# Running both mixers before both feed-forward stages in a two-block trunk kernel

## The chip, the cores and the metric

The kernel runs on one core of a Trainium2 chip. The metric is the device time of one execution in microseconds, as the median of several runs. The engines are named as in the profile: PE (matrix multiplications), DVE, ACT and POOL (elementwise work), SP (issues transfers).

## The reference, cut to what matters

One layer over 2048 rows of width 1024, all in float32:

```python
def reference(x, ...):
    for l in range(L):                       # L = 1
        xn = rmsnorm(x, norm1_g[l])
        z = xn @ w_in[l]
        u_pool, zq, zf, zi, zo, zg = split(z)
        gates = sigmoid(zg + b_gate[l])      # two gates of width 1024
        ya = pool_mixer(u_pool, ...) @ w_pa[l]
        yb = hgrn2_mixer(zq, zf, zi, zo, ...) @ w_pb[l]
        x = x + (gates[:, 0] * ya + gates[:, 1] * yb) @ w_o[l]
        x = x + conv_glu_ffn(rmsnorm(x, norm2_g[l]), ...)   # w_up, causal conv of width 3, SiLU gate, w_down
    return rmsnorm(x, final_g)
```

The pooling, the recurrence of `hgrn2_mixer` and the convolution look only backwards along the rows, so a later block needs states and last rows of an earlier one, and no FFN result is needed by a mixer (there is one layer).

## The kernel before, in words

The rows are worked on as two super-blocks of 1024 rows, `b0` = 0 and 2, each made of two halves of 512 rows (blocks 0, 1 and 2, 3). A super-block goes through `mixer(b0)` and `ffn(b0)`, and the program runs mixer 0, FFN 0, mixer 2, FFN 2.

Inside `mixer`, the input projections come first (tiles `io`, `fr`, `gr` and others), beside them the tasks of the pooling and of the recurrence. Their results are spilled to DRAM as `md` and `od` and come back as `mx` and `oT`, which the branch projections `pa` and `pb` split into a high and a low part (`mxs_0h`, `mxs_0l`, `oTs_0h` and so on). The output projection `wo` follows, in seven products in the order P1, P6, P5, P7, P4, P3, P2. After P4 the finished rows x + mixer of the first half exist, after P2 those of the second. `ffn` has the up-projection (`up`), the convolution and gate, and the down-projection (`dn`), again in seven products, the last ones P4 and P3, each followed by the final norm of its rows.

Each large product of super-blocks is done by seven smaller products over sums of operands, and each of those by three matrix multiplications over high and low parts. The weights come through one stream in the order in which the products use them: SP loads `raw` (8 buffers), ACT casts it to the high part (L205) and DVE subtracts for the low part (L206), both into `ops`. The order of this stream is written down ahead by `plan_mixer` and `plan_ffn`.

Sums of weights that the products of `wo`, `up` and `dn` need are built in DRAM by transfers alone (`Sums.make`, started by `prepare`): a copy on ACT's queue (L278) or an accumulating transfer on POOL's (L275), 1 MB in most steps, ten groups of eight steps, two groups at a time. `wo` is `sw`, `up` is `su0` to `su5`, `dn` is `sd0` to `sd2`. After a step the builder waits `SUM_LAG` ticks, where a tick is six matrix multiplications. It starts after the first `io` projection.

The next stage's operands are made while the last products of a stage run. `forms_of(kind, b, ...)` makes them in two tasks (first half and second half): `norm_rows` takes the root of the mean square of each row (on ACT, `row_rstd`, L626, with a few small steps on POOL), scales the row with it on DVE (L640), PE transposes it (L646) and ACT copies it back with the norm's gain (L654); then come the splits (L597 on ACT, L598 on DVE). `"x"` is the operand of a mixer and `"m"` that of an FFN. In before, `forms_of("m", b0)` begins in `wo` behind P7 and takes its rows from SBUF; `spill_rows` stores them to DRAM afterwards (`dx`), since `dn` adds them later. `forms_of("x", b0 + 2)` begins in `dn`'s P3 at k = 1, where `load_rows` fetches x (L501), and again at k = 4 for the second half. `go_io` and `go_up` let the second half's transposes begin.

All tiles of 512 columns share a ring of 77 buffers (`slot`), and the engines' instructions run on each engine in the order in which the program writes them.

Of the kernel before, what the change touches and what calls it, by code (L numbers as in the profile page):

```python
# [11 lines left out]
F32 = mybir.dt.float32  # L12
# [59 lines left out]
SUM_LAG = 7  # L72
# [6 lines left out]
def tile_trunk(  # L79
# [409 lines left out]
    for n in range(SEQ // SB):  # L489
        plan_mixer(n)  # L490
        plan_ffn()
# [13 lines left out]
    def load_rows(b):  # L505
        for j in range(NT):
            load_x_tile(b, j)
# [122 lines left out]
    def norm_rows(src, name, xs, after, lag=1):  # L630
        for j in range(NT):
            while (src, j) not in ready:
                yield 1
            halves = [xt[src, j, c] for c in range(2)]
            t = [slot(f"{name}xs{j}_{hf}") for hf in range(2)]
            r = row_rstd(halves, t, f"{name}{j}")
            if lag:
                yield lag
            for hf in range(2):
                dve.tensor_scalar(t[hf], halves[hf], r[:, 0:1], None, ALU.mult)  # L640
                xs[j, hf] = t[hf]
            after(j)
# [14 lines left out]
    def spill_rows(b):  # L657
        def after(j):
            for hf in range(2):
                t = xt.pop((("m", b), j, hf))  # L660
                d = dram.tile([P, 512], F32, tag=f"dx{b}_{j}_{hf}", name=f"dx{b}_{j}_{hf}")
                sp.dma_start(d, t)
                x2d[b, j, hf] = d
        return after

    def forms_a_task(src, gain, forms, full, after=lambda j: None, early=False):
# [4 lines left out]
        def rows(j):  # L671
            after(j)
            if early:
                for k in range(KD):
                    transpose(pts[k], xs, j, k)
# [10 lines left out]
    def forms_b_task(src, gain, forms, full, after, go):  # L686
        name = f"{src[0]}{src[1]}_"
        xs = {}
        yield from norm_rows(src, name, xs, after, 0)
# [54 lines left out]
    def forms_of(kind, b, gain, after=lambda b: lambda j: None, early=False, go=lambda: True):  # L744
        forms = {k: [] for k in ("B11", "B21", "B22", "T1", "T2", "T3", "T4")}
        full = {k: [] for k in ("B11", "B21", "T2")}
        first = Task(forms_a_task((kind, b), gain, forms, full, after(b), early))
        late = Task(forms_b_task((kind, b + 1), gain, forms, full, after(b + 1), go))
        return forms, first, late
# [408 lines left out]
    def mixer(b0, forms, late):  # L1158
# [172 lines left out]
        def ready_rows(hf):  # L1331
            def done(j):
                for c in range(2):
                    xt[("m", b0 + hf), j, c] = acc[hf, j, c]
                ready.add((("m", b0 + hf), j))
# [11 lines left out]
        go_up[0] = False  # L1347
        return nxt
# [3 lines left out]
    def ffn(b0, forms, late):  # L1352
# [162 lines left out]
        go_io[0] = False  # L1515
# [73 lines left out]
```

## Time and profile before

| | |
|---|---|
| time, median of 3 runs | 2622.06 us (2621.85 to 2622.27) |
| profiled execution, first to last instruction | 2614.3 us |
| around the span, median less span | 7.8 us (the profile gives no time of its own for the execution beside the span) |
| mean granted clock of TensorE | 0.989 |
| PE busy | 2533.7 us, 97% |
| DVE, ACT, POOL busy | 75%, 45%, 35% |
| HBM read, written | 384.94 MB, 187.17 MB |

The stages by PE's timeline, from the start of the span: mixer 0 from 16 to 671 us (`pa` from 464.5, `wo` from 579.5), FFN 0 to 1339 (`dn` from 1111), mixer 2 to 1950 (`pa` from 1763, `wo` from 1865), FFN 2 to 2606 (`dn` from 2389), and the last rows' norm to 2614.

The busy line tells only that PE has nearly no time to spare over the whole. Where it has some is read from stretches: two stages that do the same work in the two super-blocks can be laid side by side, and what differs between them is a wait or the clock. In a timeline row, the bracket at the end holds the idle time of that engine before the instruction and what ended it. DMA landing times run from the issue to the last byte.

### The profile page before, as it was taken

What the parts mean: (1) busy time and instruction counts of PE and PEld (TensorE: products, weight loads), DVE (VectorE), ACT (ScalarE), POOL (GpSimd) and SP (SyncE); (2) the same over time, 40 slices, a digit from 0 to 9 for tenths busy, and PEclk for the clock granted to TensorE, in tenths of its full rate; (3) what the DMA queues carried; (4) which work ended last, traced back from release to release, by engine and by line L of the source; (5) the groups of instructions that cost most, each with busy time, mean ns of one, the idle gap of its engine ahead of it and who ended that gap; (6) DMA issues with size and microseconds to landing.
All of it is one profiled execution on the core that took longest, in us unless ns stands there. A gap on an engine that the chain in (4) does not pass through costs nothing. (4 is left out here: it accounts for less than half of the span.)

```text
span 2614.3 us, 35569 instructions
## 1 busy us (share of the span) xinstructions
PE 2533.7 (97%) x11464; PEld 2064.8 (79%) x11464; DVE 1967.4 (75%) x3390; ACT 1168.9 (45%) x2204; POOL 909.3 (35%) x1253
## 2 busy tenths in 40 slices
PE   7899999989999999999999999999999999999998
PEld 6788888767778888878878788887787888887887
DVE  7898779358799877876476787774778987787845
ACT  5333434224555544555364344442345554445633
POOL 5544343062444343362141111200623433335402
PEclk9999999999999999999999999999999999999999
DMA  6887868888778897587365344346452445545943
GB/s 221 274 213 211 224 189 242 268 275 214 198 188 241 243 240 198 165 305 255 108 195 157 101 135 121 116 145 218 142 173 84 151 150 148 141 141 185 377 142 105
DMA packets 254059, 496.90 MB, mean 190 GB/s; under 512 B 26736, under 2 KB 43248, under 8 KB 253552
## 3 DMA queue, kind: packets, MB, share of 16 engines
q1 hardware_dynamic: 187968, 319.89, 38.9%
q0 software_dynamic: 41504, 110.64, 16.6%
q10 hardware_dynamic: 24400, 64.08, 7.1%
q8 instruction: 91, 1.49, 0.2%
q14 instruction: 96, 0.79, 0.1%
HBM read 384.94 MB, written 187.17 MB: 219 GB/s over the span
## 5 line engine op out<-in xcount | busy, mean ns | idle before, releaser
L205 ACT CAST ops<-raw 128x512 fp32r<-128x512 f32 x732 | 451.6, 620 | 780.1 <-PE dn_P L145 141.1
L206 DVE TENSOR_TENSOR ops<-raw,ops 128x512 fp32r<-128x512 f32 x732 | 564.1, 775 | 214.2 <-ACT ops L205 208.7
L1381 DVE SCALAR_TENSOR_TENSOR e<-h,cols,e 128x512 f32<-128x512 f32 x176 | 142.4, 813 | 29.9 <-ACT e L1379 26.1
L1379 ACT ACTIVATE e<-h,cols 128x512 f32<-128x512 f32 x176 | 142.6, 814 | 24.2 <-DVE h L984 16.9
L1384 DVE SCALAR_TENSOR_TENSOR e<-h,cols,e 128x512 f32<-128x512 f32 x176 | 133.9, 769 | 3.0
L796 POOL DMA_DIRECT2D g_P<-dg_P x154 | 83.7, 545 | 107.6 <-PE dn_P L145 70.0
L1090 POOL TENSOR_TENSOR gf_P<-e,e 128x512 f32<-128x512 f32 x44 | 67.8, 1542 | 153.1 <-DVE e L1390 97.8
L1090 POOL TENSOR_TENSOR gf_P<-gf_P,e 128x512 f32<-128x512 f32 x44 | 60.1, 1366 | 68.5 <-DVE e L1390 68.1
L1374 POOL COPY h<-h 128x2 f32<-128x2 f32 x88 | 40.7, 482 | 113.9 <-DVE h L982 112.0
L1301 POOL TENSOR_TENSOR ya<-ya,gl 128x512 f32<-128x512 f32 x32 | 45.8, 1460 | 98.4 <-issue 49.1
L1376 POOL COPY hist<-h 128x2 f32<-128x2 f32 x88 | 35.3, 401 | 127.3 <-DVE h L984 125.6
L1234 ACT ACTIVATE gt<-gt,cols 128x512 f32<-128x512 f32 x48 | 34.8, 724 | 90.5 <-DVE gt L984 71.1
L1388 ACT ACTIVATE e<-e 128x512 f32<-128x512 f32 x88 | 55.5, 631 | 37.9 <-DVE e L1384 37.4
L984 DVE TENSOR_TENSOR h<-up_u,up_V 128x512 f32<-128x512 f32 x88 | 60.2, 684 | 15.2 <-PE up_V L145 14.8
L1197 POOL TENSOR_TENSOR q<-q,qs 128x512 f32<-128x512 f32 x16 | 22.5, 1407 | 136.0 <-ACT qs L1196 105.0
L846 POOL COPY qm<-q 128x64 f32<-128x64 f32 x64 | 22.4, 367 | 117.0 <-DVE q L852 21.6
L1066 DVE TENSOR_TENSOR x<-x,wo_P 128x512 f32<-128x512 f32 x88 | 56.4, 690 | 6.2 <-PE wo_P L145 6.1
L1066 DVE TENSOR_TENSOR ac<-ac,dn_P 128x512 f32<-128x512 f32 x72 | 46.6, 683 | 13.4 <-PE dn_P L145 13.3
L1404 POOL DMA_DIRECT2D dg_P<-gf_P x88 | 52.5, 596 | 10.9 <-POOL gf_P L1090 6.5
L1450 POOL TENSOR_TENSOR fss<-fss 128x1 f32<-128x1 f32 x16 | 4.6, 289 | 141.5 <-ACT fj L1439 141.5
L619 POOL TENSOR_SCALAR ro<-so 128x4 f32<-128x4 f32 x16 | 5.2, 323 | 135.6 <-ACT sq L956 135.4
L1018 ACT COPY up_e<-up_X 128x512 f32<-128x512 f32 x44 | 25.8, 586 | 56.7 <-PE up_X L145 51.6
(1265 smaller groups left out, 8332.4 us busy)
## 6 DMA issues: line engine op xcount, KB each, us to landing
g_P<-dg_P POOLq DMA_DIRECT2D x154, 256.0 KB, 6.2
raw<-in_w_up_t SPq DMA_DIRECT2D x132, 256.0 KB, 3.3
raw<-in_w_in_t SPq DMA_DIRECT2D x98, 256.0 KB, 3.3
dg_P<-gf_P POOLq DMA_DIRECT2D x88, 256.0 KB, 3.9
raw<-in_w_io SPq DMA_DIRECT2D x68, 256.0 KB, 4.9
dg_P<-e SPq DMA_DIRECT2D x66, 256.0 KB, 3.3
raw<-in_w_dn SPq DMA_DIRECT2D x66, 256.0 KB, 3.0
x<-in_x SPq DMA_DIRECT2D x64, 256.0 KB, 5.3
```

What stands on the lines that cost most here:

```text
L205: self.mark = act.copy(hi, v)
L206: dve.tensor_tensor(lo, v, f32(hi), ALU.subtract)
L796: eng.dma_start(t, d)
L984: dve.tensor_tensor(dst, t, ps, ALU.add if how == "add" else ALU.subtract)
L1066: dve.tensor_tensor(t, t, ps[j], ALU.add if sg > 0 else ALU.subtract)
L1090: pin(pool.tensor_tensor(t, x0, x1, op))
L1301: pool.tensor_tensor(y[m, hf], y[m, hf], g, ALU.add)
L1379: in_turn(act.activation(t, h[:, 2:], AF.Identity, bias=col(o_cb + mt), scale=col(o_cw + 4 * MF + mt)))
L1381: in_turn(second(dve.scalar_tensor_tensor(t, h[:, 1 : 1 + TB], col(o_cw + 2 * MF + mt), t, ALU.mult, ALU.add)))
L1384: dve.scalar_tensor_tensor(t, h[:, 0:TB], col(o_cw + mt), t, ALU.mult, ALU.add)
L1388: in_turn(act.activation(g, g, AF.Silu))
L1404: pool.dma_start(d, t)
```

## The change

The main loop runs the two mixers first and then the two FFNs, and the weight stream is planned in that order. `wo` of the first mixer is now followed by `io` of the second, `wo` of the second by `up` of the first FFN, and `dn` of the first by `up` of the second. Finished rows no longer stay in SBUF for the FFN: `keep_rows` takes the root of each row tile as soon as the tile is done, copies it into a small tile that stays on chip (`rs2`, 128x16), and stores the rows to DRAM. `norm_rows` for `"m"` fetches them and scales them with the kept root. The next operands begin in `wo` at P4, k = 0 (`begin`), for the first mixer x of block 2 with block 3's loads at P3, k = 0 (`begin2`), for the second the rows of block 0. In `dn` of the first FFN, `each3` begins the rows of block 2 in place of x. `SUM_LAG` goes from 7 to 11.

```diff
-SUM_LAG = 7
+SUM_LAG = 11
...
     for n in range(SEQ // SB):
         plan_mixer(n)
+    for n in range(SEQ // SB):
         plan_ffn()
...
     def norm_rows(src, name, xs, after, lag=1):
+        kind, b = src
         for j in range(NT):
-            while (src, j) not in ready:
+            if kind == "m":
+                halves = [fetch(x2d[b, j, c], f"{name}r{j}_{c}") for c in range(2)]
+                t, r = halves, rs2[:, b * NT + j : b * NT + j + 1]
                 yield 1
-            halves = [xt[src, j, c] for c in range(2)]
-            t = [slot(f"{name}xs{j}_{hf}") for hf in range(2)]
-            r = row_rstd(halves, t, f"{name}{j}")
-            if lag:
-                yield lag
+            else:
+                ...
             for hf in range(2):
-                dve.tensor_scalar(t[hf], halves[hf], r[:, 0:1], None, ALU.mult)
+                dve.tensor_scalar(t[hf], halves[hf], r, None, ALU.mult)
...
+    rs2 = const.tile([P, SEQ // P], F32, tag="rs2", name="rs2")
+
+    def keep_rows(b, j, halves):
+        junk = [slot(f"mj{b}_{j}_{c}") for c in range(2)]
+        r = row_rstd(halves, junk, f"m{b}_{j}")
+        pool.tensor_copy(rs2[:, b * NT + j : b * NT + j + 1], r[:, 0:1])
+        for c in range(2):
+            d = dram.tile([P, 512], F32, tag=f"dx{b}_{j}_{c}", name=f"dx{b}_{j}_{c}")
+            sp.dma_start(d, halves[c])
+            x2d[b, j, c] = d
...
+        def begin(k):
+            if k == 0:
+                if last:
+                    nxt.append(forms_of("m", 0, o_n2, go=lambda: go_up[0]))
+                else:
+                    load_rows(b0 + 2)
+                    nxt.append(forms_of("x", b0 + 2, o_n1, go=lambda: go_io[0]))
+
+        def begin2(k):
+            if k == 0 and not last:
+                load_rows(b0 + 3)
...
         wo.run("P7", 2)
-        nxt = forms_of("m", b0, o_n2, spill_rows, go=lambda: go_up[0])
-        wo.run("P4", 2, done=ready_rows(0))
-        wo.run("P3", 2)
-        wo.run("P2", 3, done=ready_rows(1))
-        go_up[0] = False
-        return nxt
+        go_io[0] = go_up[0] = False
+        wo.run("P4", 2, begin, rows_done(0))
+        wo.run("P3", 2, begin2)
+        wo.run("P2", 3, done=rows_done(1))
+        return nxt[0]
...
         def each3(k):
             if k == X_AT and not last:
-                load_rows(b0 + 2)
-                nxt.append(forms_of("x", b0 + 2, o_n1, go=lambda: go_io[0]))
-            if k == X_AT2 and not last:
-                load_rows(b0 + 3)
+                nxt.append(forms_of("m", b0 + 2, o_n2, go=lambda: go_up[0]))
...
-    for b in range(0, SEQ // TB, 2):
-        forms, task, late = nxt
-        join(task)
-        forms, task, late = mixer(b, forms, late)
-        join(task)
-        nxt = ffn(b, forms, late)
+    for stage in (mixer, ffn):
+        for b in range(0, SEQ // TB, 2):
+            forms, task, late = nxt
+            join(task)
+            nxt = stage(b, forms, late)
```

What the change does to the order of instructions shows in three places. Line numbers of the changed kernel are some eight higher there; a name's number behind the last underscore only tells tiles apart, and `mxs1_2h` is the split of the third `mx` tile of block 1.

The first is ACT at the first mixer's `pa`, where the reloaded tiles are split while copies of weight sums (`su`) are issued. Before:

```order
L597 CAST mxs1_0h_4836<-mx1_0_4834 128x512
L205 CAST ops131_4940<-raw117_4632 128x512
L278 DMA su1s4_3375<-su1s2_3373 16x16384
L956 ACTIVATE sq0_3_4855,so0_3_4856<-po0_3_4846 128x128 x4
L1234 ACTIVATE gt0_1_7_4876<-gt0_1_7_4876,cols_84 128x512
L791 DMA gd0_1_7_4879<-gt0_1_7_4876 128x512
L205 CAST ops132_5003<-raw118_4634 128x512
L278 DMA su2s4_3497<-su2s2_3495 16x16384
L597 CAST mxs1_1h_4894<-mx1_1_4892 128x512
L1234 ACTIVATE gt1_0_7_4904<-gt1_0_7_4904,cols_84 128x512
L791 DMA gd1_0_7_4907<-gt1_0_7_4904 128x512
L597 CAST mxs1_2h_4911<-mx1_2_4909 128x512
```

And the same place in the changed kernel:

```order
L205 CAST ops131_4931<-raw117_4620 128x512
L278 DMA su1s3_4551<-in_w_up_t 512x1x512
L598 CAST mxs1_0h_4827<-mx1_0_4825 128x512
L964 ACTIVATE sq0_3_4846,so0_3_4847<-po0_3_4837 128x128 x4
L1242 ACTIVATE gt0_1_7_4867<-gt0_1_7_4867,cols_84 128x512
L205 CAST ops132_4994<-raw118_4622 128x512
L799 DMA gd0_1_7_4870<-gt0_1_7_4867 128x512
L598 CAST mxs1_1h_4885<-mx1_1_4883 128x512
L1242 ACTIVATE gt1_0_7_4895<-gt1_0_7_4895,cols_84 128x512
L799 DMA gd1_0_7_4898<-gt1_0_7_4895 128x512
L598 CAST mxs1_2h_4902<-mx1_2_4900 128x512
```

Two copies stood between the first and the third split, and now one stands ahead of the first.

The second is ACT at the end of the first `wo`, where P2's splits stand among the squares of rows. Before, the squares were those of finished rows (`m0`):

```order
L626 ACTIVATE m0_xs2_0_6239,m0_2ss_6241<-x0_2_0_5443 128x512
L626 ACTIVATE m0_xs2_1_6240,m0_2ss_6241<-x0_2_1_5445 128x512
L597 CAST wo0_P2_0h_6253<-ya1_4_5044 128x512
L205 CAST ops168_6306<-raw154_6066 128x512
L626 ACTIVATE m0_xs3_0_6274,m0_3ss_6276<-x0_3_0_5487 128x512
L626 ACTIVATE m0_xs3_1_6275,m0_3ss_6276<-x0_3_1_5489 128x512
L597 CAST wo0_P2_1h_6296<-ya1_5_5132 128x512
L205 CAST ops169_6331<-raw155_6092 128x512
L597 CAST wo0_P2_2h_6317<-ya1_6_5259 128x512
```

In the changed kernel the squares of block 3's x, which wait for loads, stand there:

```order
L627 ACTIVATE x3_xs0_0_6360,x3_0ss_6362<-x3_0_0_6329 128x512
L627 ACTIVATE x3_xs0_1_6361,x3_0ss_6362<-x3_0_1_6331 128x512
L627 ACTIVATE x3_xs1_0_6371,x3_1ss_6373<-x3_1_0_6333 128x512
L627 ACTIVATE x3_xs1_1_6372,x3_1ss_6373<-x3_1_1_6335 128x512
L627 ACTIVATE x3_xs2_0_6382,x3_2ss_6384<-x3_2_0_6337 128x512
L627 ACTIVATE x3_xs2_1_6383,x3_2ss_6384<-x3_2_1_6339 128x512
L205 CAST ops171_6506<-raw157_6112 128x512
L278 DMA su1s4_4552<-su1s2_4550 16x16384
L627 ACTIVATE x3_xs3_0_6393,x3_3ss_6395<-x3_3_0_6341 128x512
L205 CAST ops172_6546<-raw158_6149 128x512
L627 ACTIVATE x3_xs3_1_6394,x3_3ss_6395<-x3_3_1_6343 128x512
L598 CAST wo0_P2_2h_6410<-ya1_6_5248 128x512
```

Eight squares of freshly loaded rows and one copy now stand ahead of the split `wo0_P2_2h`. They come from the end of the first `dn`, where before eight squares of `x3` stood between `dn0_P3_9h` and `dn0_P3_10h`; there the changed kernel has

```order
L598 CAST dn0_P3_9h_18416<-g0_P3_9_18228 128x512
L598 CAST dn0_P3_10h_18437<-g0_P3_10_18272 128x512
L205 CAST ops575_18522<-raw561_18287 128x512
L661 ACTIVATE m2_b0_18474<-m2_t0_18469,cols_84 128x512
L205 CAST ops576_18631<-raw562_18318 128x512
```

with the two splits side by side.

The third is POOL at the second mixer's `pb`, where `ro` belongs to the end of the recurrence and `ya` is the first merge of a branch. Before:

```order
L619 TENSOR_SCALAR ro2_3_16895<-so2_3_16890 128x4
L620 TENSOR_TENSOR ro2_3_16895<-ro2_3_16895,neghalf_116 128x4
L619 TENSOR_SCALAR ro3_3_17005<-so3_3_17000 128x4
L620 TENSOR_TENSOR ro3_3_17005<-ro3_3_17005,neghalf_116 128x4
L1301 TENSOR_TENSOR ya2_0_17008<-ya2_0_17008,gl2_1_0_17365 128x512
```

In the changed kernel:

```order
L620 TENSOR_SCALAR ro2_3_10819<-so2_3_10814 128x4
L621 TENSOR_TENSOR ro2_3_10819<-ro2_3_10819,neghalf_116 128x4
L275 DMA su5s1_10172<-in_w_up_t 256x1x512
L620 TENSOR_SCALAR ro3_3_10929<-so3_3_10924 128x4
L621 TENSOR_TENSOR ro3_3_10929<-ro3_3_10929,neghalf_116 128x4
L275 DMA sd0s1_10359<-in_w_dn 512x1x512
L275 DMA su5s3_10174<-in_w_up_t 256x1x512
L275 DMA sd0s3_10361<-in_w_dn 512x1x512
L1309 TENSOR_TENSOR ya2_0_10932<-ya2_0_10932,gl2_1_0_11292 128x512
```

Four accumulating transfers have moved here, three of them together.

More of the change, by code (lines that the diff above doesn't have):

```diff
@@ L655, in transposed, with forms_a_task @@
         return t
[L657 to L666, printed above, removed]
+    rs2 = const.tile([P, SEQ // P], F32, tag="rs2", name="rs2")
[7 more added lines that the diff above has]
+            x2d[b, j, c] = d
+    def forms_a_task(src, gain, forms, full, early=False):
         name = f"{src[0]}{src[1]}_"
@@ L684, in forms_a_task, with forms_b_task @@
             forms[key].append(split(t, f"{name}f{k}", True))
-    def forms_b_task(src, gain, forms, full, after, go):
+    def forms_b_task(src, gain, forms, full, go):
         name = f"{src[0]}{src[1]}_"
         xs = {}
-        yield from norm_rows(src, name, xs, after, 0)
+        yield from norm_rows(src, name, xs, lambda j: None, 0)
         while not go():
```

25 lines of the change are left out of this document (15 added, 10 removed).

## The prediction

> **What bounds the kernel now.** I read the busy line of the page first, then the busy times by stage, then the list of waits, and last the timeline around each long wait. The profiled span is 2614.3 us; the runs have a median of 2622.06 us, 7.8 us more, which lies around the span and which I leave as it is. So a microsecond off the span is a microsecond off the time.
>
> ```profile
> PE 2533.7 (97%) x11464; PEld 2064.8 (79%) x11464; DVE 1967.4 (75%) x3390; ACT 1168.9 (45%) x2204; POOL 909.3 (35%) x1253
> ```
>
> TensorE is the bound, and the change leaves its 11464 matmuls alone. What can move is the idle rest, 81 us, and the stretches at half clock behind it. The stages (start:end, length, busy of PE, PEld, DVE, ACT, POOL, granted clock, DMA share, GB/s) show where they lie:
>
> ```profile
> 464.50:671.00 206.50, 187.47 (x814) 149.59 (x813) 131.66 (x198) 68.71 (x142) 69.20 (x69) 0.97 0.86 254
> 1111.20:1338.80 227.60, 221.02 (x957) 178.99 (x956) 143.25 (x223) 111.77 (x216) 80.80 (x140) 0.99 0.67 227
> 1763.40:1950.30 186.90, 181.04 (x814) 146.56 (x813) 123.69 (x194) 66.97 (x140) 61.05 (x61) 1.00 0.55 178
> 2389.40:2606.00 216.60, 214.84 (x925) 173.40 (x923) 134.67 (x204) 99.44 (x186) 72.53 (x121) 1.00 0.60 208
> ```
>
> Rows one and three are the same work (pa, pb and wo, 814 matmuls): the first mixer needs 19.6 us more, at a DMA share of 0.86 against 0.55. Rows two and four are the down-projections: the first needs 11.0 us more. In PE's timeline (start, length, instruction, in brackets the idle time before it and what ended it) these are the longest waits outside io, and below them the list of all that PE waits for in the second mixer's pa, pb and wo (us in total, times, longest):
>
> ```profile
> 486.57 0.80 PE L145 MATMUL pa<-mxs_2h,ops 128*128 128x512 f32 x1 [5.83 <-ACT mxs_2h L597]
> 534.22 0.49 PE L145 MATMUL pb<-oTs_0h,ops 128*128 128x512 f32 x1 [4.01 <-ACT oTs_0h L597]
> 585.83 1.53 PE L145 MATMUL wo_P<-ops,wo_P_0l 128*128 128x512 f32 x4 [4.16 <-DVE wo_P_0l L598]
> 1331.59 3.78 PE L145 MATMUL dn_P<-ops,dn_P_10h 128*128 128x512 f32 x8 [4.14 <-ACT dn_P_10h L597]
> ...
> PE wo_P L145 <- DVE x L1066: 2.9, 2, 1.6
> PE pt L968 <- DVE ot L962: 1.7, 1, 1.7
> PE wo_P L145 <- ACT wo_P_0h L597: 1.2, 1, 1.2
> ```
>
> The first three lie in the first mixer's pa, pb and wo, and the second mixer has none of them. The fourth is at the end of dn0, where x of the next super-block is loaded.
>
> **The contention in the first mixer.** The reloads mx and oT (md and od in DRAM back to SBUF) feed pa and pb. Four answers on these tiles, in the order mx first mixer, mx second, oT first, oT second:
>
> ```profile
> DMA to landing us min/median/max: 3.1/8.5/10.5
> ...
> DMA to landing us min/median/max: 3.4/3.7/5.5
> ...
> DMA to landing us min/median/max: 5.5/6.3/9.7
> ...
> DMA to landing us min/median/max: 3.6/4.1/5.4
> ```
>
> What else is under way: the copies of the weight sums (L278, 1 MB each) and the accumulates on POOL (L275). Their issue times (first and last start) and an accumulate's landing:
>
> ```profile
> L278 ACTq DMA_DIRECT2D su1s<-su1s x2: 476/508/540, 421.9 to 472.1; - x2
> L278 ACTq DMA_DIRECT2D su2s<-su2s x2: 475/486/497, 429.8 to 475.4; - x2
> L278 ACTq DMA_DIRECT2D su3s<-in_w_up_t x2: 550/570/590, 516.3 to 542.3; - x2
> L278 ACTq DMA_DIRECT2D su4s<-in_w_up_t x2: 566/568/571, 523.4 to 550.6; - x2
> ...
> DMA to landing us min/median/max: 3.9/6.7/10.1
> sd0s<-in_w_dn POOLq DMA_DIRECT2D x4, 1024.0 KB, 12.2
> ```
>
> The pa wait that ends at 486.57 stands behind copies issued at 472.1 and 475.4, the pb wait that ends at 534.22 behind copies issued at 516.3 and 523.4. In the second mixer the sums are long done.
>
> **The change part by part.**
>
> T1, dn0's end. The timeline of ACT and then of PE:
>
> ```profile
> 1324.24 0.63 ACT L626 ACTIVATE x_xs<-x 128x512 f32<-128x512 f32 x1 [2.30 <-DMA x<-in_x]
> 1324.78 0.19 ACT L626 ACTIVATION_READ_ACCUMULATOR x_xs<-x 128x1 f32 x1
> 1330.94 0.60 ACT L597 CAST dn_P_10h<-g_P 128x512 fp32r<-128x512 f32 x1
> ...
> 1323.58 0.60 PE L646 MATMUL x_t<-ident,x_xs 128*128 128x128 f32 x4
> 1323.93 0.72 PE L145 MATMUL dn_P<-ops,dn_P_8l 128*128 128x512 f32 x2
> 1324.49 2.04 PE L145 MATMUL dn_P<-ops,dn_P_9h 128*128 128x512 f32 x8
> ```
>
> The split dn_P_10h stands behind eight squares of x3, and the first waits for a load. The changed kernel has no squares here: 16 fetches of finished rows and 16 DVE scalings by a root that is on chip, and dn_P_10h directly behind dn_P_9h. The wait of 4.14 goes, with the half clock behind it (eight matmuls took 3.78 after it and 2.04 before). Against dn2, dn0 has 32 transposes more, some 2.8 us at 0.35 for four (1323.58 to 1323.93); 11.0 less 2.8 leaves 8.2 as the most to gain. Nothing is gained if the fetches come as late as x did. In place of x, finished rows are now late if anything is, and then PE waits for their transposes. I take -7, ends -8.2 and 0.
>
> T2, wo0's end. This is where the x loads, 16 squares and 16 scalings now are, so what is taken from dn0 comes here. The eight x3 loads stand on SP behind the stores of the finished rows, and eight x3 squares stand on ACT ahead of the splits wo0_P2_2h and 2h's follower 3h. Behind those wait the casts of the weights and then PE. From before: the last of the eight row stores of the first half, the cast that must now wait, and the first matmul that needs it; then the landing of x and of the row stores:
>
> ```profile
> 646.98 1.61 SPq L662 DMA_DIRECT2D dx<-x  x3
> 649.85 0.61 ACT L597 CAST wo_P_2h<-ya 128x512 fp32r<-128x512 f32 x1
> 661.13 0.62 PE L145 MATMUL wo_P<-ops,wo_P_2h 128*128 128x512 f32 x2
> ...
> DMA to landing us min/median/max: 4.3/5.5/6.5
> ...
> DMA to landing us min/median/max: 2.0/6.0/14.0
> ```
>
> x3 is issued from 648.6 on; with 5.5 us the first lands at 654 and, at eight squares of 0.63 and their read-outs of 0.19, the split starts at 661 and PE waits about 0.5 to 1.5; with the 14.0 that one store took it waits about 9. I take +2.5, nearer the median than the maximum, ends 0 and +10.
>
> Does a wait of 2 us also cost clock? Two waits in the second mixer's projections, and the two windows of 3.4 us around the later one:
>
> ```profile
> 1447.23 1.13 PE L895 MATMUL pl<-q,k 128*128 128x128 f32 x8 [1.21 <-DVE q L820]
> 1450.00 0.77 PE L145 MATMUL gr_X<-x_f4h,ops 128*128 128x512 f32 x1 [1.64 <-ACT gr_e L1018]
> ...
> 1446.80:1450.20 3.40, 1.33 (x9) 1.17 (x10) 3.40 (x8) 2.67 (x7) 0.00 (x0) 0.98 0.75 200
> 1450.20:1453.60 3.40, 3.40 (x9) 2.66 (x10) 3.40 (x10) 0.03 (x1) 0.32 (x1) 0.52 0.24 70
> ```
>
> PE is busy for 1.33 of 3.40, and the next 3.4 us run at a granted clock of 0.52: 1.6 us lost. I count that half window for each wait of T2, T4 and T5. The Trainium skill ("TensorE: Matmul & The Clock Gate", section on HAM oscillation) puts the rule as no PE-idle gaps above about 3.4 us; by that rule T2's wait would cost no clock and the sum would be some 1.5 us lower, but this row shows the clock falling after gaps that are each at most half as long, so the row decides.
>
> T3, wo2's end. m0 and m1 are fetched back from DRAM, 16 fetches of 256 KB, on SP behind the row stores. In the second mixer's wo the DMA share is low (0.55 over the row above), and x_b and square work is the same as before. 0, ends -1 and +3. The chain of transposes and T2 forms at the start of both up-projections stands as it did, so its waits stay.
>
> T4, thinner sums in the first mixer. A step now comes every 11 ticks instead of 7. Between mxs_0h and wo's first split ACT had six copies, now three, and none among the oT splits. The window behind the pa wait, and DVE ahead of the wo wait:
>
> ```profile
> 487.60:491.00 3.40, 3.40 (x9) 2.60 (x9) 3.11 (x8) 1.17 (x6) 0.00 (x0) 0.51 0.73 265
> ...
> 579.00 4.28 DVE L206 TENSOR_TENSOR ops<-raw,ops 128x512 fp32r<-128x512 f32 x1 [1.04 <-ACT ops L205]
> ```
>
> pa: 5.8 of wait and, at 0.51 from 486.57 to 491, about 2.2 of clock; one copy ahead in place of two, landing between 8.5 and 3.7, so 3 stays: -5. pb: 4.0 and 1.7; no copy near, oT lands near 4.1 and was 6.3: -4.5. wo: 4.2 and 1.7 come from the weight subtraction of 4.28 us on DVE, which the order of both engines still allows: -2. Sum -11.5, taken as -11; ends 0 and -19.6, the whole difference of rows one and three.
>
> T5, the same sums in the second mixer. They now run through it and into up0. Copies stand before mxs2_0h and mxs2_1h, none before mxs3 or among the oT splits; but three accumulates stand together on POOL ahead of pb2, and two copies ahead of wo2. Half of what pb lost in the first mixer, 3, and 1 for wo: +4; ends 0 and +19.6.
>
> Edits that I cost at nothing: 32 more fetches (8 MB, issued at the two stage ends of T1 and T3, where their landing is counted), 16 root copies of 128x1 on POOL (35% busy), the other order of weights in the stream, and the missing x-square wait at io2. Squares, scalings and stores are as many as before. If their cover goes, it shows in T1 to T3.
>
> Sum: -7 + 2.5 + 0 - 11 + 4 = -11.5; span 2602.8, time 2610.5 us.
>
> **The rivals.**
>
> R1, one copy delays a reload as long as two do. For: the second copy was issued 3.3 us after the first, less than the shortest landing of 3.9, so the two overlapped for most of the wait. Then pa keeps its wait, T4 is -6 and the time 2615.5. The Trainium skill ("DMA: Bandwidth & Descriptors", section on queues, rings and completion order) says each DMA engine takes turns between the queue rows that have work; by that, one copy on ACT's row slows SP's reload as much as two. Against: the second mixer without copies waits for nothing, so a shorter overlap should gain something.
>
> R2, dn0's stall moves whole to wo0. The order there is the same (eight x3 squares ahead of a split), and loads there landed later. T2 is then +9, the time 2617, no change that can be told.
>
> R3, slower. Three accumulates, each about 12 us to land, stand on POOL ahead of the oT reloads of the second mixer. If these land as late as the 14.0 of the slowest store, 10 above their 4.1, pb waits about 10 at each of its two halves, and with 1.7 of clock each and 3 for pa and wo T5 is +26: 2632.5. It decides from T5 at +20.7. Against: in the first mixer accumulates also stood there and cost far less.
>
> R4, all contention goes: T4 -19.6, T5 0, the time 2598.
>
> **How the numbers follow.** 0.2%, 5.2 us, is about what a measurement of this kernel can tell from no change. Forecast (2604 to 2615) 0.45, R1 0.13, R2 0.13, R3 0.14, R4 0.15. Faster takes R4, half of R1 (which lies at the bound) and the forecast but 0.05 for its upper tail: 0.60. Same takes R2 and those two rests: 0.24. Slower is R3 and 0.02 for several ends at once: 0.16. The range goes from 2599, beside R4, to 2629, between before and R3.
>
> **What would show it.** T1: no wait for dn_P_10h, dn0 near 220 us. T2: a wait for wo_P_2h below 3 us. T4: pa to wo of the first mixer near 195 us, oT landing near 4. T5: the second near 191. It is wrong if the second mixer shows the waits for mxs or oTs that the first had, or if wo0 waits above 6.

## The result, and the profile after

The changed kernel takes 2650.86 us (median of 4 runs, 2646.61 to 2654.49) against 2621.95 us of the kernel before beside it: 1.0112 times as long, 95% interval 1.0097 to 1.0126. That is 28.9 us slower; the forecast was 11.5 us faster, and the time lies above its range.

The profiled execution took 2654.49 us with a span of 2652.8, so 1.7 us lie around the span. The 38.5 us between the two spans are therefore more than the 28.9 between the medians: this execution was 3.6 us above its median, and the profiled one of before, if 1.7 us lay around its span too, some 6 us below. Stage lengths come from one execution of each kernel, so a difference of a few us between two of them can be that of the executions.

The busy line of the page after:

```profile
PE 2544.8 (96%) x11464; PEld 2065.4 (78%) x11464; DVE 1973.7 (74%) x3390; ACT 1166.7 (44%) x2202; POOL 915.8 (35%) x1269
```

PE executes the same 11464 matmuls and is busy for 11.1 us more than before: that part of the 38.5 is matmuls at a lower clock or with operands that come late, the rest is idle time. The stages of after, in the order first projections, pa to wo of the first mixer, pa to wo of the second, dn0, up2, dn2 (same columns as in the prediction):

```profile
119.80:479.10 359.30, 344.47 (x1718) 285.59 (x1716) 288.68 (x670) 135.45 (x304) 132.97 (x145) 0.99 0.63 185
479.10:686.70 207.60, 185.29 (x814) 147.13 (x812) 138.07 (x198) 73.65 (x163) 77.20 (x87) 0.97 0.79 235
1111.80:1318.70 206.90, 189.90 (x814) 149.51 (x813) 133.63 (x207) 68.83 (x144) 71.17 (x75) 0.95 0.73 222
1758.90:1978.30 219.40, 217.65 (x957) 176.65 (x956) 140.85 (x220) 100.31 (x181) 69.76 (x114) 1.00 0.68 233
1978.30:2426.70 448.40, 437.35 (x1884) 351.96 (x1883) 369.64 (x516) 227.05 (x373) 163.70 (x248) 0.99 0.47 142
2426.70:2644.30 217.60, 214.45 (x925) 173.20 (x923) 134.12 (x204) 99.50 (x186) 72.41 (x121) 1.00 0.61 207
```

And two stages of before that the prediction did not show, the first projections and up2:

```profile
116.20:464.50 348.30, 341.43 (x1717) 284.43 (x1716) 287.39 (x667) 134.09 (x302) 140.81 (x151) 1.00 0.80 221
1950.20:2389.40 439.20, 434.82 (x1882) 351.58 (x1881) 363.19 (x510) 223.99 (x362) 156.34 (x237) 1.00 0.47 141
```

Against before, dn0 is 8.2 us shorter, as said. The first projections are 11.0 longer, the first mixer's pa to wo 1.1 longer instead of 11 shorter, the second's 20.0 longer, and up2 9.2 longer. The long waits of PE in after:

```profile
600.93 2.08 PE L145 MATMUL wo_P<-ops,wo_P_0l 128*128 128x512 f32 x4 [12.29 <-DVE wo_P_0l L599]
...
1136.20 0.79 PE L145 MATMUL pa<-mxs_3h,ops 128*128 128x512 f32 x1 [5.80 <-ACT mxs_3h L598]
...
1981.79 0.50 PE L145 MATMUL up_X<-m_f1l,ops 128*128 128x512 f32 x1 [2.30 <-DVE m_f1l L599]
...
1991.31 0.76 PE L145 MATMUL up_X<-m_f4h,ops 128*128 128x512 f32 x1 [4.30 <-ACT up_e L1026]
```

**The wait of 12.29 at wo0.** Before it was 4.16. DVE and then POOL in after, just ahead of it:

```profile
563.68 9.51 DVE L206 TENSOR_TENSOR ops<-raw,ops 128x512 fp32r<-128x512 f32 x1
...
579.53 0.69 DVE L1301 TENSOR_TENSOR gl<-gl,pb 128x512 f32<-128x512 f32 x1 [5.74 <-DMA gl<-gd]
...
583.00 4.00 DVE L206 TENSOR_TENSOR ops<-raw,ops 128x512 fp32r<-128x512 f32 x1
...
595.37 0.69 DVE L1301 TENSOR_TENSOR gl<-gl,pb 128x512 f32<-128x512 f32 x1 [7.17 <-DMA gl<-gd]
...
599.25 1.62 DVE L599 TENSOR_TENSOR wo_P_0l<-ya,wo_P_0h 128x512 fp32r<-128x512 f32 x1
```

```profile
561.47 1.14 POOL L275 DMA_DIRECT2D su1s<-in_w_up_t  x1
562.14 1.80 POOL L1098 TENSOR_TENSOR yf_P<-ya,ya 128x512 f32<-128x512 f32 x1
...
569.61 3.01 POOL L1098 TENSOR_TENSOR yf_P<-ya,ya 128x512 f32<-128x512 f32 x2
```

A weight subtraction, which takes 0.68 us where nothing holds it, took 9.51. It began 1.5 us into a run of eight additions on POOL that followed an accumulate's issue, and ended 0.56 us after the last of them (572.63). A second one, at 583.00, took 4.00: it followed the accumulate that POOL issued at 581.53, and it too ended 0.56 us after the last of POOL's three additions there (586.45). Behind each of them everything is in order: the next weight load on SP waits for that subtraction's buffer, and gates `gl` stand behind the load. SP's issues:

```profile
559.15 14.38 SPq L182 DMA_DIRECT2D raw<-sw0s  x2
...
577.57 9.78 SPq L182 DMA_DIRECT2D raw<-sw0s  x2
...
588.40 0.86 SPq L804 DMA_DIRECT2D gl<-gd  x2
```

And of the list of SP's waits from 537 to 605 us (total, times, longest) the first row:

```profile
SPq L182 <- DVE ops L206: 37.7, 7, 13.7
```

SP waited up to 13.7 us (7.3 at the same place before), until the first hold ended at 573.19. The gates behind that load were issued at 574.5 to 577.0, DVE waited 5.74 for one, and only then came to the subtraction of 4.00. The next load waited for this one until 587.0, the gates behind it were issued at 588.4 and 588.9, DVE waited 7.17 for the first, `wo_P_0l` came at 599.25 and PE at 600.93. So two holds, one behind the other, make the wait of 12.29.

**The wait of 5.80 in the second mixer.** ACT's row ahead of it:

```profile
1135.53 0.62 ACT L598 CAST mxs_3h<-mx 128x512 fp32r<-128x512 f32 x1 [6.64 <-DMA mx<-md]
```

And the landing of `mx` there, issued from 1096.0 to 1126.4:

```profile
DMA to landing us min/median/max: 3.0/4.9/9.1
```

The last fetch, issued at 1126.4, took 9.1 us. This looks like the contention of the first mixer: an accumulate had been issued at 1123.9. Whether the sums are the cause is what a11q2 below tries.

**Up2.** The rows of `m2` are fetched behind the stores of the final norm. SP in after:

```profile
1952.20 2.17 SPq L1480 DMA_DIRECT2D out<-fo  x3
...
1956.87 0.86 SPq L1480 DMA_DIRECT2D out<-fo  x2
1957.83 0.42 SPq L804 DMA_DIRECT2D m_r<-dx  x1
...
1964.78 4.94 SPq L804 DMA_DIRECT2D m_r<-dx  x8
```

All sixteen start between 1957.8 and 1969.4, dn0 ends at 1978.3, and the waits at 1981.79 and 1991.31 follow.

### The profile page after: what moved, and what is told of

Its sections match the earlier page's. It is cut to its first block, busy times and chain, and to the rows that moved or that the text cites. A ratio compares the mean times of both kernels' runs of the same rounds, so it can differ in the third digit from the quotient of the medians.

```text
span 2652.8 us, 35625 instructions
## 1 busy us (share of the span) xinstructions
PE 2544.8 (96%) x11464; PEld 2065.4 (78%) x11464; DVE 1973.7 (74%) x3390; ACT 1166.7 (44%) x2202; POOL 915.8 (35%) x1269
## 3 DMA queue, kind: packets, MB, share of 16 engines
q0 software_dynamic: 41504, 110.64, 16.4%
## 4 chain that ended last, share of the span: by engine, by line
PE 78%; DVE 8%; DMA 7%; issue 3%; ACT 2%; POOL 2%; SPq 1%; DVEq 0%; ACTq 0%; POOLq 0%
PE up_Z L145 13%; PE dn_P L145 13%; PE up_V L145 9%; PE up_X L145 9%; PE gr_Z L145 4%; PE wo_P L145 4%; PE pa L145 3%; PE gr_X L145 3%; PE gr_V L145 3%; DVE ops L206 2%; PE fr_Z L145 2%; PE pb L145 2%; PE pl L867 1%; PE fr_X L145 1%; PE fr_V L145 1%
## 5 line engine op out<-in xcount | busy, mean ns | idle before, releaser
L206 DVE TENSOR_TENSOR ops<-raw,ops 128x512 fp32r<-128x512 f32 x732 | 571.0, 783 | 220.0 <-ACT ops L205 212.3
L867 PE MATMUL pl<-qm,k 128*128 128x192 f32 x256 | 47.8, 336 | 4.3 <-DVE qm L858 4.1
```

What stands on the lines that cost most here:

```text
L206: dve.tensor_tensor(lo, v, f32(hi), ALU.subtract)
L867: pe.matmul(pa_[:, c * 192 : c * 192 + 192], ks[:, (i + c) * P : (i + c + 1) * P], mv[:, c].rearrange("p s x -> p (s x)"), start=True, sto ...
```

## Experiments

The time of each kernel is compared with the kernel before on the same chip (median 2618 to 2623 us). "Minus" and "plus" are these differences, +28.9 for the changed kernel. Stage lengths run from the start of one stage's matmuls to the next in the profiled execution; pa is counted from where the last projection has ended, some 8 to 10 us later than in the windows above.

| us | proj 0 | pa to wo, 1st | pa to wo, 2nd | dn0 | up2 |
|---|---|---|---|---|---|
| before | 357.9 | 196.8 | 178.8 | 227.6 | 439.2 |
| after | 368.4 | 198.5 | 198.3 | 219.4 | 448.3 |
| a7 | 360.3 | 202.0 | 181.3 | 220.2 | 450.3 |
| b11 | 364.5 | 198.6 | 178.3 | 258.8 | 438.6 |
| a7q | 357.6 | 180.7 | 184.5 | 219.3 | 450.7 |
| a7qx | 356.6 | 180.4 | 184.5 | 220.0 | 438.5 |

### Lag and order apart: a7 and b11

The main theory (S) was that the lag did the harm, the rival (O) that the new order did. a7 is the changed kernel, b11 the kernel before, each with the other's lag.

```diff
 # a7: after            # b11: before
-SUM_LAG = 11           -SUM_LAG = 7
+SUM_LAG = 7            +SUM_LAG = 11
```

> The changed kernel with SUM_LAG back at 7; all else of the change stays. Theory S (the slower pace of the weight sums is the loss: it shifts where copies and accumulates stand in the first mixer and pushes others into the second mixer's pa, pb and wo): the first mixer returns to before's order up to wo's P4, so projections near 348 us and pa to wo near 206, the second mixer's pa to wo falls from 199 to 187-190, dn0 stays near 219 and up2 near 448; total near 2622, within 4. Rival O (the stage order itself is the loss: x loads at wo0's end, rows fetched back, up2's start): the total stays at 2645 or more, since only the first mixer's small part moves.

a7: 2630.28 us (6 runs), +9.6, ratio 1.0036 [1.0023, 1.0049]. The lag is worth 19 of the 28.9 us and the order the other 9.6: neither theory alone. Two of a7's windows, the second mixer and up2:

```profile
1107.00:1294.20 187.20, 179.67 (x801) 144.19 (x800) 128.29 (x198) 66.40 (x139) 63.05 (x68) 1.00 0.60 199
1955.10:2405.30 450.20, 439.68 (x1883) 353.05 (x1881) 369.40 (x516) 226.94 (x373) 164.62 (x248) 0.99 0.46 141
```

At lag 7 the last accumulate is issued at 1064.8, ahead of the second mixer's pa at 1107; in after they run on to 1576.9. Without them the second mixer is nearly as quick as before (the +2.5 lie in wo2, 87.7 after 85.0). Up2's loss stays: it belongs to the order.

> The kernel before with SUM_LAG 11 alone, stage order as before. Theory S: the first mixer is that of the changed kernel: projections near 359 us (348 before), pa and pb together near 98 (105), a wait near 12 us before the first wo product (4), wo near 100; total 2622 + 11 - 7 + 8 = 2634. Rival O: the pace alone changes nothing that can be told, 2618 to 2626, and the 11 us in the projections belong to the new stage order.

b11: 2662.22 us (4 runs), +41.5, ratio 1.0158 [1.0143, 1.0173], far above both numbers. Its long waits over the whole run:

```profile
PE dn_P L145 <- ACT dn_P_0h L597: 14.2, 1, 14.2
PE wo_P L145 <- DVE wo_P_0l L598: 11.5, 2, 10.8
```

In the first mixer b11 does what after does (wait 10.8, 198.6 us against 198.5), and up to wo's P4 the two programs give SP, DVE, POOL and ACT the same order: there the lag alone acts. The rest of the miss is dn0 (+31.2), which neither theory had. It starts at 1126.3, and the last accumulates of its sums `sd1` and `sd2` are issued at 1190.3 and 1192.3. Of SP's waits around its start the row of the weight loads:

```profile
SPq L182 <- DMA sd1s<-in_w_dn: 28.5, 1, 28.5
```

In the old order the thinner sums are not done when dn0 wants them; in the new one the second mixer lies ahead of dn0. So a lag of 11 costs 41.5 us in the old order and 19.3 in the new: the two parts of the change do not simply add.

### Sums paused in the mixers: a7q and a11q2

`prepare` gives no step while a flag is set, from the start of `pa` to the end of `wo`.

```diff
+    quiet = [False]
...
+            while quiet[0]:
+                yield 1
             g = active.pop(0)
...
                     mtask = Task(pa_task())
+                    quiet[0] = True          # a11q2: b0 > 0
...
         wo.run("P2", 3, done=rows_done(1))
+        quiet[0] = False
```

> As a7, and no step of the weight sums is issued from the start of the reloads for pa to the end of wo, in both mixers; the rest of the sums runs later, up to up0. Theory S: the sums' traffic makes pa, pb and wo of the first mixer slow: 206 falls to 187-192, total 14 to 18 us less than a7. Rival A (the waits come from how SP's loads, DVE and POOL are lined up there, not from the traffic): pa and pb gain some 8 but wo keeps its wait of 4 us or more, total at most 9 us less than a7.

a7q (a7 with the pause): 2612.09 us (5 runs), -8.6, ratio 0.9966 [0.9953, 0.9979], 18.2 below a7. The first mixer's window:

```profile
474.00:654.70 180.70, 172.85 (x767) 138.44 (x765) 122.47 (x186) 69.36 (x149) 71.03 (x81) 1.00 0.58 194
```

21.3 us shorter than in a7, at a DMA share of 0.58 and full clock: nearly all that this place lost is due to the sums. The profiled execution of a7 was 4.2 us above its median and that of a7q 4.3 below, so the 18.2 between the medians is the safer size. Where the sums went no stage got longer (second projections 350.3 us in both, up0 439.5 against 440.7). The second mixer, where none is issued in either kernel, takes 3.1 us more in a7q; why is not shown.

> The changed kernel (SUM_LAG 11), with no step of the weight sums issued from the reloads for pa to the end of wo in the second mixer; they follow in up0. The first mixer is untouched. Theory S (the second mixer lost its 11 us in pa, 3 in pb and 5 in wo to the sums that moved into it): pa to wo of the second mixer falls from 198 to 186-190, total 9 to 13 us less than the changed kernel (the sums now end just ahead of dn0, which may give back up to 3). Rival: the rows' stores and fetches of the new order make pa to wo slow; then it stays above 195.

a11q2 (after, paused only in the second mixer): 2641.18 us (4 runs), +23.0, ratio 1.0087 [1.0072, 1.0102]; the second mixer takes 183.3 us instead of 198.3. Its waits for `mxs_2h` and `mxs_3h` are gone. So the moved sums cost 15 us there, and the rest of its loss is in wo2, as in a7. The total fell by 5.9 only, not by the 9 to 13 expected: in the profiled executions dn0, up2 and dn2 with the last rows' norm came out 2.4, 2.4 and 3.5 us longer than in after.

### Who holds the subtraction: a11d and a11b

a11d moves the additions `yf` from POOL to DVE:

```diff
-            pin(pool.tensor_tensor(t, x0, x1, op))
+            pin((eng or pool).tensor_tensor(t, x0, x1, op))
...
-                add_forms(two, yf, k, f"yf{b0}")
+                add_forms(two, yf, k, f"yf{b0}", eng=dve)
```

> The changed kernel (SUM_LAG 11), with the additions of the operand forms in pb (yf, 16 in each mixer) on DVE in place of POOL. Theory P (a weight subtraction of DVE was held for 9.5 us while POOL ran eight additions without a break; SP's next weight load waited for that buffer, the gate loads behind it, and so wo's first split): with POOL's runs halved no L206 there is held above 4 us, the wait before the first wo product falls from 12.3 to 2 or less, wo of the first mixer from 100 to below 90, total 10 to 14 us less than the changed kernel. Rival Q (the gate loads are late by the traffic of the sums alone): the wait stays at 10 or more and the total within 4 us.

a11d: 2634.05 us (4 runs), +15.9, ratio 1.0053 [1.0035, 1.0072], 13 better than after. The weight subtractions of pb and wo of its first mixer (durations in ns):

```profile
L206 DVE TENSOR_TENSOR ops<-raw,ops x35: 674/683/1776, 539.8 to 671.9; 128x512 fp32r<-128x512 f32 x35
```

And what is left of PE's wait:

```profile
PE wo_P L145 <- DVE wo_P_0l L599: 3.8, 1, 3.8
```

No subtraction above 1.78 us, wo0 88.1 instead of 100.2; the wait is shorter but not at the 2 or less expected. An addition that had moved to DVE was held in its turn: 3.15 us at 557.99, behind an accumulate issued at 556.85 and until 0.56 us after POOL's two additions there. But in a7q, too, none was above 1.77, with the additions on POOL. What a7q lacked were the accumulates, which POOL issues. a11b parts the two: after, with the pause only from the start of the first mixer's pb to the end of P5 of its wo.

```diff
+        quiet[0] = b0 == 0
         branch("pb", 1, oT, evac_b, load_res)
...
         for p in ("P1", "P6", "P5"):
             wo.run(p)
+        quiet[0] = False
```

> The changed kernel at lag 11 with the sums paused only from the start of the first mixer's pb to the end of P5 of its wo, so that POOL issues no accumulating transfer there and keeps its additions of ya and yf. Theory H (a weight subtraction on DVE is held for POOL's whole run of additions only where the run follows a transfer that POOL has just issued): no L206 in pb and wo above 2 us although POOL's additions still stand back to back, the wait for wo_P_0l 1.5 us or less instead of 12.3, wo0 86 to 89 us instead of 100.2, time 13 to 17 us below the changed kernel. Rival N (a run of additions on POOL alone holds DVE): an L206 of 7 us or more stays, wait 8 or more, wo0 96 or more, time within 5 us of the changed kernel. The first projections should stay near 366 to 369 us, since the lag there is untouched.

The subtractions of a11b from pb to the end of wo:

```profile
L206 DVE TENSOR_TENSOR ops<-raw,ops x35: 672/681/1396, 537.7 to 670.1; 128x512 fp32r<-128x512 f32 x35
```

And POOL's additions, the first row and one near the end of the run:

```profile
547.56 5.86 POOL L1312 TENSOR_TENSOR ya<-ya,gl 128x512 f32<-128x512 f32 x4 [46.40 <-DVE gl L1304]
...
588.73 1.74 POOL L1101 TENSOR_TENSOR yf_P<-ya,ya 128x512 f32<-128x512 f32 x1
```

POOL adds without a gap for over 40 us, with no transfer issued between, no subtraction takes more than 1.40, and the wait for `wo_P_0l` is gone; wo0 takes 89.2 us (86 to 89 was said). H held for the mechanism: in pb and wo the long hold came with a run of additions behind an accumulate, and not with the additions alone. It missed on the time, which came where N had put it: 2647.72 us (4 runs), +27.1, ratio 1.0098 [1.0081, 1.0115], within 3 of after. pa to wo of the first mixer fell by 12.7 us, but wo2 rose by 2.0, with a subtraction held there 3.70, up2 by 4.2 and dn2 with the last rows' norm by 2.0 in the profiled executions, and after's was its slowest run. The sums that were held back were issued later and cost again; which of them cost what was not tried.

The condition in H is too narrow in one point: the transfer need not be one of the sums. In after, at the end of dn0, where the last accumulate lies 371 us back, POOL issues a fetch and then makes two products of 128x512 tiles. POOL's issue, and the subtraction on DVE:

```profile
1947.84 0.61 POOL L804 DMA_DIRECT2D g_P<-dg_P  x1
...
1948.06 3.67 DVE L206 TENSOR_TENSOR ops<-raw,ops 128x512 fp32r<-128x512 f32 x1
```

In the profiles of before, after and the twelve experiments, 106 subtractions take more than 1.9 us. Every one of them began within 4.3 us of an issue on POOL (34 times of a sum, 72 times of another fetch or store) and ended 0.55 to 0.56 us after an addition or product of 128x512 tiles on POOL. Of the 1429 that ran beside such work of POOL more than 4.4 us behind any issue, none took more than 1.89. An issue close by is not enough: 108 others had one within 4.4 us and took at most 1.81.

### Up2: a7f, a7qn, a7qx and a7qxf

`FIN_WAIT` delays the final norm of dn0's second half.

```diff
-FIN_WAIT = 4
+FIN_WAIT = 20
```

> As a7, and the final norm of dn0's last rows (squares fj on ACT) begins 20 ticks after its rows are done instead of 4, so that up2's first copies of its products (up_e) stand ahead of the squares on ACT. Theory: these squares make the 4.3 us wait at up2's start; with its half clock about 6 us less than a7, up2 near 442. Rival: the wait of 2.3 before it, from DVE's additions and weight subtractions, and the clock behind it carry the 9 us; then it is within 2 us of a7.

a7f: 2630.18 us (5 runs), +9.5, ratio 1.0036 [1.0023, 1.0049]: no gain. Up2 takes 451.1; the wait for `up_e` shrinks and another comes. The rival had the time right, but the new wait is for `m_T30l`, not the one for `m_f1l` that it named (1.8 in a7 as in a7f):

```profile
PE up_Z L145 <- DVE m_T30l L599: 2.8, 1, 2.8
PE up_X L145 <- ACT up_e L1026: 1.9, 1, 1.9
```

a7qn is a7q without the final norm of the 512 rows of dn0's second half; they are stored as they are.

```diff
         def final(hf, j):
             if hf == 1 and not last:
                 yield FIN_WAIT
+                for c in range(2):
+                    ...
+                    sp.dma_start(out[rr : rr + P, 512 * c : 512 * c + 512], t)
+                return
```

> As a7q (SUM_LAG 7, sums paused from pa to wo), and the final norm of dn0's second half is left out: these 512 rows are stored as they are. Theory N (the norm's squares on ACT and scalings on DVE and POOL, which before ran beside io2, take ACT and DVE where up2's operand chain needs them, and moving them by 20 ticks only moved the waits): up2 falls from 451 to 439-441 as up0, total 10 us less than a7q. Rival: the rows' fetches, scalings and additions at dn0's end make m_f1l and up_e late without the norm; then up2 stays at 446 or more.

a7qn: 2609.24 us (5 runs), -8.9, ratio 0.9963 [0.995, 0.9976], against -8.6 of a7q. Up2 falls by 4.6 only, to 446.1, and keeps 3.2 for `m_f1l` and 1.9 for `up_e`: the norm has a part in the loss, but the operands are late without it too.

a7qx begins the fetch of `m2` one product earlier, in P4 at k = 6 instead of P3 at k = 1.

```diff
-            if k == X_AT and not last:
+            if k == X_AT4 and not last:          # X_AT4 = 6
...
-        down.run("P4", 2, done=lambda j: Task(final(0, j)))
         go_up[0] = False
-        down.run("P3", 6 if last else 3, each3, lambda j: Task(final(1, j)))
+        down.run("P4", 2, each3, done=lambda j: Task(final(0, j)))
+        down.run("P3", 6 if last else 3, done=lambda j: Task(final(1, j)))
```

> As a7q (SUM_LAG 7, sums paused from pa to wo), and the rows of block 2 and 3 for up2 are fetched and scaled from dn0's P4, k = 6 on instead of P3, k = 1, so that the 16 fetches no longer stand on SP behind the stores of the finished rows of P4. Theory L (at dn0's end the fetched rows land last, DVE scales them beside P3's additions, and up2's first splits and copies are late for it: 9 to 11 us): up2 falls from 451 to 441-443, dn0 stays at 219-221, total 7 to 10 us less than a7q, 2602 to 2605. Rival M (ACT's squares of the final norm ahead of up_e are enough to hold up2): the wait for up_e stays at 4 us, up2 at 446 or more.

a7qx: 2599.29 us (4 runs, 2595.91 to 2600.92), -23.5, ratio 0.9915 [0.989, 0.9941]. Up2's window:

```profile
1931.50:2370.10 438.60, 434.23 (x1882) 351.01 (x1881) 363.70 (x510) 222.32 (x361) 155.22 (x235) 1.00 0.47 145
```

And the two longest of PE's waits there:

```profile
PE up_Z L145 <- ACT m_T23h L601: 1.8, 1, 1.8
PE up_Z L145 <- DVE m_T23l L602: 0.7, 1, 0.7
```

438.6 us, as before the change, and `m_f1l` and `up_e` are no longer waited for: L was right, and the gain larger than it said. dn0 keeps its 220.0. This is the fastest kernel of the study. The fetches in a7q and in a7qx (last two numbers before the semicolon: first and last start):

```profile
L807 SPq DMA_DIRECT2D m_r<-dx x16: 319/342/425, 1909.1 to 1920.2; - x16
...
L807 SPq DMA_DIRECT2D m_r<-dx x16: 319/372/383, 1828.2 to 1852.8; - x16
```

In a7q they begin 20.5 us ahead of up2 (1929.6), in a7qx 103.3 ahead of it (1931.5). The edit moves them by six of the eleven steps of a product, some 17 us at the 30.6 us that a product takes (an estimate). That they come 80 us earlier fits L: in a7qx no store that waits for finished rows stands ahead of them on SP.

> As a7qx, with the final norm of dn0's second half begun after 20 ticks instead of 4. Theory L: the earlier fetch has done it, the norm now stands in the operand chain, and up2 is as in a7qx or up to 3 us longer. Rival M: only the two together free up2; it is 4 us or more shorter than in a7qx.

a7qxf (a7qx with `FIN_WAIT` 20): 2606.35 us (4 runs), -16.4, ratio 0.9944 [0.9921, 0.9966], up2 446.9. Neither theory had it: up2 is 8.4 us longer than in a7qx, and PE waits 2.9 for `m_T30l` (2.8 in a7f). So the short delay is right; that the delayed norm now stands in the operand chain is likely, and no run takes it apart.

### Denser sums in the old order: b4q and b5q

Before, with the pause of a7q and a lag of 4 or 5, so that the sums are done in time for dn0.

```diff
-SUM_LAG = 7
+SUM_LAG = 4        # b5q: 5
```

> The kernel before, stage order as before, with the sums paused from pa to the end of wo and SUM_LAG 4 so that they still end ahead of dn0. Theory S: pa to wo of the first mixer falls from 206 to 186-190; denser sums cost the first projections 0 to 5 us more; total 2604 to 2609, so better than the changed order with the same pause (2612). Rival: the pause gains only with the new order; then 2616 or more.

b4q: 2627.4 us (7 runs), +9.3, ratio 1.0044 [1.0029, 1.0059]. Pa to wo is short (184.7 us), but the first projections take 389.9, 32 more than before. Their window:

```profile
117.10:507.00 389.90, 363.23 (x1762) 300.78 (x1761) 305.10 (x683) 142.18 (x320) 150.07 (x162) 0.96 0.91 253
```

And PE's longest waits there:

```profile
PE pl L898 <- DVE q L823: 9.4, 3, 4.3
PE pl L862 <- DVE qm L853: 6.3, 4, 4.0
```

That denser sums cost the projections 0 to 5 us was wrong: at a DMA share of 0.91 the recurrence is waited for, and the clock falls to 0.96. The profiled execution lies 9.3 us above the median, so the 32 is rather too large. The total came where the rival had put it, but not for its reason: the pause gains in the old order too.

> The kernel before, sums paused from pa to the end of wo, SUM_LAG 5 (they still end ahead of dn0). If the new order itself costs 9.6 us at equal pace (a7 against before), the old order with the same pause comes to 2612 - 10 = 2602, with the first projections near 358 as at SUM_LAG 7. Rival: what made them 390 at SUM_LAG 4 is the denser sums, and at 5 they are still at 365 or more; then 2610 or more.

b5q: 2606.13 us (4 runs), -16.6, ratio 0.9944 [0.9922, 0.9966]; first projections 371.5, as the rival said, pa to wo 176.5. The total lies between the two theories, and shows what the old order can give when the sums are placed well: with the pause alone the new order is behind it (a7q, -8.6), and with the earlier fetch as well 6.8 us quicker on the same chip (a7qx).

## Why the prediction was wrong, point by point

The forecast was -11.5 us and +28.9 came. Of the 40.4 between them, a7 puts 26.3 at the lag of the sums (T4 and T5: -7 said, +19.3 came) and 14.1 at the order (T1 to T3: -4.5 said, +9.6 came). The steps that failed are T5, whose size was wrong by 15.5, the first projections, which have no term, wo in T4, and the sentence in T3 that the waits at the start of the up-projections stay. Both signs of being wrong that it named came: the second mixer waits for `mxs` (5.80) and wo0 waits above 6 (12.29).

- **T1**: right. The wait for `dn_P_10h` is gone, and dn0 lost 8.2 us, the end that was named as the most to gain. What the step left out is what follows it: it named the transposes as late next, but put no price on them in up2, and T3's sentence that the chain "stands as it did, so its waits stay" failed. The sixteen fetches stand on SP behind the final stores, and up2 lost 9.1 (after) and 11.1 (a7). At lag 7 as at 11 this cancels the gain, and a7qx, with the fetches ahead of the stores, has up2 at its old length.
- **T2** and **R2**: `wo_P_2h` was not waited for in after, and for 1.2 in a7. Between before and a7 wo0 grew by 3.5, near the +2.5. R2's 9 did not come.
- **T3**: wo2 grew by 2.7 in a7, near the +3 end, and by 4.2 in a7q and a11q2, beyond it, where 0 was taken.
- **T4**: half right. The reloads land as early as it said (mx 4.1 us in the median, oT 4.0), and pa fell by 4.2 us and pb by 2.8 (said: 5 and 4.5). For wo -2 was taken and +8.7 came (91.4 to 100.2). The step saw that DVE's subtraction of 4.28 was allowed by the order of both engines, but treated its size as fixed; in after two of them, of 9.51 and 4.00, and the gate loads queued behind them on SP make 12.29 of wait. It is no chance of one execution: b11 and a11q2, with the same order there, have 9.50 and 9.52.
- **The term that is missing**: the first projections, +10.5 us at lag 11. They were taken as unchanged although every sum in them moved. Five lag-11 kernels with the same order there take 364.5 to 369.4 us, so up to 4 of the 10.5 can be this execution's.
- **T5**: the size was wrong. +4 was said, and the second mixer lost 19.5, beside its upper end of 19.6 (15 by a11q2 for the sums, the rest in wo2). The waits are in pa (5.80) and spread (clock 0.95), where "none before mxs3" was argued from ACT's copies; the accumulate on POOL was not counted against `mx`.
- **R3**, the slower rival, had the right stage, and of its 26 us 19.5 came, but not at its place: the oT reloads cost 1.6 of wait, not 10 at each half. Its direction alone would not have sufficed: 2632.5 is still 18 below the time. **R1** and **R4** did not come: pa kept 1.5 of its 5.83 of wait.
- **7.8 us around the span**: wrong, 1.7 us lie there in after, and 1.8 to 1.9 in the runs of before beside the experiments. The profiled execution was some 6 us below the median. The forecast does not suffer from it, since the 7.8 was added back and the sum so started from the median.

By stages after less before: projections +10.5, first pa to wo +1.7, second +19.5, dn0 -8.2, up2 +9.1, and the rest (io's start, io, second projections, dn2) +5.9, in all 38.5, the difference of the spans. By edits: from +28.9 the lag of 7 takes 19.3, the pause 18.2 and the earlier fetch 14.9 (12.2 of them show in up2), which gives the -23.5 of a7qx.

One thing stays open. The projections' loss at lag 11 has no single long wait. The longest of after there, and of before:

```profile
PE pl L867 <- DVE qm L858: 4.1, 2, 2.2
PE pl L903 <- DVE q L828: 3.5, 2, 2.4
PE ur_Z L145 <- DVE ur_u L1028: 2.0, 1, 2.0
```

```profile
PE pl L895 <- DVE q L820: 1.7, 1, 1.7
```

With the lag the stage takes 389.9 (4, in an execution 9.3 above its median), 371.5 (5), 356.4 to 360.3 (7) and 364.5 to 369.4 us (11), so it is not a matter of density alone. That small DVE operations are held beside POOL's additions and transfers at other places then is likely from the trace, but no run here takes it apart.

## What to carry to other kernels

Background transfers are not free just because an engine or a queue has room on average: place them by the stage that hides them, and pause them where operands are reloaded just in time. A change of their rate moves all of them, so price every stage that they enter or leave, also the ones that the change does not name. And when a stall is taken from one stage's end, look at what feeds the start of the next: the gain is kept only if its operands are fetched earlier too.

## What the runs showed of the hardware

A DVE subtraction with both inputs in SBUF (0.68 us) was held until POOL's run of additions had ended, 9.51 us over eight of them, where POOL had just issued a transfer at the head of the run. The holds of 4.00 us in after, 3.84 and 4.28 in before and 3.70 in a11b end at the same 0.56 us after POOL's last addition, and an accumulate had been issued at most 4.3 us earlier; behind a fetch, at the end of dn0 in after, it was 3.67. Without such an issue POOL added for over 40 us and no subtraction took more than 1.40 (a11b). The Trainium skill ("SBUF — State Buffer", section "Who interferes with whom") says that a DVE instruction with two SBUF inputs contends with a GpSimd instruction that reads SBUF, and that the ports which they share are an exclusive lock. The trace agrees that one waits for the other, but here the wait lasted over eight instructions of POOL. Why the transfer matters is not shown.
